# Layer 1's weight splits moved into layer 0, and its output projection woven into its attention

## The chip, the cores and the metric

The kernel runs on one core of one Trainium2 chip. A core has TensorE (PE in the profile, PEld for its weight loads), VectorE (DVE), ScalarE (ACT), GpSimd (POOL) and SyncE (SP). SP's, ACT's and POOL's queues start DMA transfers; 16 DMA engines carry them. The metric is the device time of one execution in microseconds, and less is better.

## The reference

Two layers, 1024 positions, 1024 channels. A layer mixes positions, adds the input times a constant, normalises, applies a squared-ReLU MLP of width 4096, and normalises again. Layer 0 mixes with gated linear attention (GLA) and with multi-head latent attention (MLA, causal, 8 heads). Layer 1 mixes with a sparse attention that keeps the 256 best keys of each query by an index score (DSA), and with a state-space part (S5) whose result passes a gate (GLU). Cut to what matters:

```python
for i in range(DEPTH):
    if i % 2 == 0:   # [GLA, MLA] @ w_out
        mix = _mixer_gla_mla(x, positions, *mixer_params[i])
    else:            # [DSA, S5 with GLU] @ w_out
        mix = _mixer_dsa_s5(x, *mixer_params[i])
    x = _layernorm(DEEPNORM_ALPHA * x + mix, ln1_g, ln1_b)
    x = _layernorm(DEEPNORM_ALPHA * x + _sq_relu_mlp(x, w1, w2), ln2_g, ln2_b)

# _mixer_dsa_s5
q, k, v, qi, ki, wi, u = _split(x @ w_in, L1_SPLITS)
o_dsa = _dsa(q, k, v, qi, ki, wi * IDX_HEADS ** -0.5)   # top-k by index score, softmax, @ v
y = gelu(_s5(u, ...));  o_s5 = y * sigmoid(y @ glu_w + glu_b)
return concatenate([o_dsa, o_s5], -1) @ w_out
```

## The kernel before

**Numbers in two parts.** A float32 factor is held as a high part that TensorE's fast format (fp32r) takes exactly and a low part, the rest. A product is three passes: high by high, high by low, low by high. Whoever wants to multiply first splits: ACT copies the high part, DVE or POOL subtracts it from the value. For weights `unit` (L617) does this. It loads a block of 128 x 1024 (`wr`, 512 KB) on SP's queue and makes four tiles of 128 x 512: `wh`, `wl` for the left half, `wh`, `wl` for the right.

**Stages.** `program` (L2135 on) goes through layer 0's projections, GLA and MLA attention (until about 440 us), its output projection `out_norm` with `l0_wo` (440 to 560), the MLP as `fc1` and `fc2` with seven products in place of eight (560 to about 1160), then layer 1: the index scores and the selection (`index`, `topk`), the projections `l1_in` (L1673), DSA in two halves of queries of 16 steps each, S5 and GLU beside it (until about 1640), `out_norm` with `l1_wo`, and the MLP again. In the attentions one step handles two blocks of 128 queries of one head (32 steps in MLA): products for the scores into PSUM, a maximum on DVE (`SM`), the exponential on ACT (`p`), transposes on TensorE (`ident,p`), a split of the transposed block (`pth` on ACT, `ptl` on DVE), the products with the values (`vv`).

**What sets the order.** Nothing is issued directly. A class records every operation, a list scheduler with a cost for each operation puts them in order for each engine, and one line (L471) then issues all. So all rows of the profile carry L471, and operations are told apart by their tiles. What is recorded together can be interleaved: `program` runs several generators side by side, some steps of one for each step of another, by the numbers in the tables at L2102 to L2117 (E0, E1, GL, GS for S5 and GLU beside DSA; SKEW for the order of `out_norm`, which starts with six blocks of the first half of the positions). An operation assigned to 'E' goes to DVE or POOL, as the scheduler decides. Each queue is in order: what stands behind a waiting instruction waits too, and a DMA's issue takes its place in the queue of its engine.

**The names that the prediction uses.** `wr`, `wh`, `wl` (weights raw, high, low); `pth`, `ptl`, `p`, `SM`, `vv`, `fold`, `rs` (attention; `rs` is a block's row sums, transposed once for each pair of heads and half of the positions, eight times in MLA); `ir` (index scores in ACT); `jv`, `ja` (counting passes of the selection on DVE and ACT); `mh`, `ml` (the mixed result, the input of `out_norm`); `iq`, `qkl` (low parts of projections).

Of the kernel before, what the change touches and what calls it, by code (L numbers as in the profile page):

```python
# [11 lines left out]
F32 = mybir.dt.float32  # L12
F32R = mybir.dt.float32r
# [460 lines left out]
P, T, N, KD = 128, 1024, 512, 8  # L474
# [26 lines left out]
def run(g, n=None):  # L501

    for i, _ in enumerate(g):
        if n is not None and i + 1 >= n:
            return


def weave(main, *others):

    for _ in main:  # L510
        for o in others:
            run(o, 1)
    for o in others:
        run(o)


class Kern:
    def __init__(self, ctx, tc, A, out, dbg=None, drams=None, at=None, made=None):

        self.tc, self.A, self.out, self.at = tc, A, out, at  # L520
        self.dbg, self.drams = dbg or {}, drams
        self.uid = 0
        self.DF = self.DS = self.ZE = 0
        self.MG = 1
        nc = self.nc = Plan(tc.nc)
        self.V, self.S, self.G, self.TE = nc.vector, nc.scalar, nc.gpsimd, nc.tensor
        self.E, self.H = Either(nc, nc.vector, nc.gpsimd), Either(nc, nc.scalar, nc.vector)
        e = ctx.enter_context
        sb, ps = e(tc.tile_pool(name="sb", bufs=1)), e(tc.tile_pool(name="ps", bufs=1, space=PSUM))
        self.pool, self.tiles = {"SB": sb, "PS": ps}, {}  # L530
        if at is not None:
            self.room = {w: p.tile([P, n // 4], F32, name=w) for w, p, n in
                         (("SM", sb, SMALL), ("PS", ps, 8 * PAGE))}
            for name, (w, o) in at.items():
                if w in ("SB", "BG"):
                    shape, dt = made[name]
                    self.tiles[name] = sb.tile(shape, dt, name=name, tag=f"{w}{o}")
# [78 lines left out]

    def unit(self, dram, he=None, le=None):  # L617

        raw = self.big(name="wr")
        self.nc.sync.dma_start(out=raw, in_=dram)  # L620
        u = []
        for i in range(2):
            wh, wl = self.slab(F32R, "wh"), self.slab(F32R, "wl")
            self.split(raw[:, i * N:(i + 1) * N], wh, wl, self.by("unit_h"), self.by("unit_l"))
            u.append((wh, wl))
        return u

    @staticmethod
    def cut(u, c, n=P):
# [555 lines left out]
        yield from self.attention([item(hd, h) for hd in range(8) for h in range(2)])  # L1185


    def out_norm(self, wname, mix, res, g, b, emit):

        V = self.V  # L1190
        us, st = {}, [{}, {}]
        for k, h in self.skewed(KD, 0, SKEW):
            if k not in us:
                us[k] = self.unit(self.A[wname][k])
            ps = self.ps1()
            self.dense(mix, h, ps, lambda kk: self.blk(us[k], kk))
# [393 lines left out]
    def topk(self, blocks, on_act, sc, hi16, lo16, bias):  # L1590
# [70 lines left out]
        for j, qb in enumerate(blocks):  # L1661
# [8 lines left out]
            bias[qb] = b  # L1670
            yield

    def l1_in(self, x, dq, dk, dv, du):  # L1673

        V, S, A, nc = self.V, self.S, self.A, self.nc
        W = A["l1_fm"]
        us = [self.unit(A["l1_v"][i]) for i in range(4)]
        for b in range(8):
            ps = self.ps1((P, 8, 64))
            bs = slice((b % 4) * P, (b % 4 + 1) * P)  # L1680
            self.tm(us, lambda k: tuple(t[:, bs] for t in x[k][b // 4]), ps)
            for hg in range(2):
                v = self.slab(F32R, "vv", (P, 4, 2, 64))
                for par in range(2):
                    src = ps[:, hg * 4 + par:hg * 4 + 4:2, :]
                    hs, ls = v[:, par::2, par, :], v[:, par::2, 1 - par, :]
                    self.copy(S, hs, src)
                    V.tensor_tensor(ls, src, hs, ALU.subtract)
                nc.scalar.dma_start(out=dv[b, hg], in_=v.rearrange("p a b c -> p (a b c)").bitcast(F32))
            yield  # L1690
        us = [self.unit(A["l1_u"][i]) for i in range(4)]
        for h in range(2):

            uq = [self.slab(name="ut", shape=(P, 8, 4, 16)) for _ in range(4)]
            for j in range(4):
                ps = self.ps1((P, 4, 8, 16))
                self.tm(us, lambda k: tuple(t[:, j::4] for t in x[k][h]), ps)
                for q in range(4):
                    self.copy(S, uq[q][:, :, j, :], ps[:, q])
                    if j == 3:  # L1700
                        nc.scalar.dma_start(out=du[q, h], in_=uq[q].rearrange("p a b c -> p (a b c)"))
                yield
# [374 lines left out]
    def glu(self, y, mix):  # L2077
# [10 lines left out]
        for h in range(2):  # L2088
            for ct in range(4):
# [12 lines left out]
RUSH, R0, NI, NT, N0, SK, ACTS, SR, E0, E1, DF, DS, E2, I2, MV, GL, GS, CI, CS, CJ, DF0, DS0, MC, WV, RO, ZE = 800, 300, 6, 2, 4, 1, (4, 7), -100, 2, 2, 0, 0, 2, 14, 3, 5, 1, 2, 2, 3, 0, 0, 4, 3, 7, 1  # L2102
# [6 lines left out]
BY = {'unit_h': 'S', 'unit_l': 'E', 'loadx_h': 'S', 'loadx_l': 'V', 'glao_h': 'S', 'glao_l': 'G', 'mlac_h': 'S', 'mlac_l': 'V', 'mlaq_h': 'S', 'mlaq_l': 'G', 'mlao_h': 'S', 'mlao_l': 'E', 'half_h': 'S', 'half_l': 'V', 'fc1_h': 'S', 'fc1_l': 'E', 'dsao_h': 'S', 'dsao_l': 'G', 'x2_h': 'H', 'x2_l': 'V', 'y_h': 'H', 'y_l': 'G', 'glu_h': 'H', 'glu_l': 'V', 'lnacc': 'G', 'lnsq': 'G', 'gla': 'G', 'gdl': 'G', 'gor': 'G', 's5u': 'V', 's5a': 'G', 's5m': 'G', 's5n': 'G', 's5t': 'G', 's5g': 'G', 'lo16': 'V', 'hi16': 'V'}  # L2109
# [25 lines left out]
def program(K, A, out, stop=None):  # L2135
    V, S, G, nc = K.V, K.S, K.G, K.nc

    def tables(name):
        S.preload_act_table_set(name)
# [5 lines left out]
    x, us = pairs(), {}  # L2145
# [47 lines left out]
    K.out_norm("l0_wo", mix, res0, "l0_ln1_g", "l0_ln1_b", K.keep("x1", op, dx))  # L2193
    if stop == "x1":
        return
    x2 = pairs()
# [56 lines left out]
        if i >= I2 and (i - I2) % E2 == E2 - 1:  # L2253
            run(s5, 1)
    run(top0)
    for i, _ in enumerate(K.dsa(dq, dk, dv, bias, mix, 0)):
        run(top1, NT)
        if i % E0 == E0 - 1:
            run(s5, 1)
    run(top1)  # L2260
    glu = K.glu(ys, mix)
    for i, _ in enumerate(K.dsa(dq, dk, dv, bias, mix, 1)):
        if i % E1 == E1 - 1:
            run(s5, 1)
        if i >= GL:
            if i == GL:
                run(s5)
            run(glu, GS)
    K.DF = K.DS = 0
    run(s5)  # L2270
    run(glu)
    if stop == "mix1":
        return
    tables("natural_log_exp_and_others")
    op = {i: [None] * 4 for i in range(1, 8)}
    K.out_norm("l1_wo", mix, res1, "l1_ln1_g", "l1_ln1_b", K.keep("x3", op, dx))

    def last(h, c, k, t):
        nc.sync.dma_start(out=out[k, :, h * N + c.start:h * N + c.stop], in_=t)
# [90 lines left out]
```

## Time and profile before

| | |
|---|---|
| time, median of 3 runs | 2386.18 us (2385.55 to 2389.04) |
| profiled execution | 2386.76 us, span 2384.6 us |
| mean granted TensorE clock | 0.991 |
| PE busy | 2299.7 us (96%) |
| DVE, ACT, POOL busy | 1765.8, 1330.2, 468.3 us |
| `wr` loads for `unit` in layer 1's mixer | 23 of 512 KB |

The span runs from the first to the last instruction; the execution's time is 2.2 us more. All times in rows are from the start of the span. A share of busy time is a mean over stages with different limits, so stages are read one by one.

### The profile page before, as it was taken

The numbers are of one execution on the slowest core, as the hardware profiler recorded it, in microseconds if no ns is written. First come the engines' busy times: TensorE is split into PE (matmuls) and PEld (weight loads), VectorE is DVE, ScalarE is ACT, GpSimd is POOL, SyncE is SP. The second block draws the span as 40 slices with busy tenths as digits, with TensorE's granted clock in tenths as the row PEclk, the third lists the DMA queues.
The fourth block names the chain that finished last, engine by engine and source line by source line (L and its number), as shares of the span: only waits on it lengthen the run. The fifth ranks groups of instructions, "written<-read, shape, count | busy, mean of one in ns | idle before, by whom it ended". The sixth has DMA issues, their size and how long they took to land. (4 is left out here: it accounts for less than half of the span.)

```text
span 2384.6 us, 33342 instructions
## 1 busy us (share of the span) xinstructions
PE 2299.7 (96%) x11356; PEld 1904.9 (80%) x11356; DVE 1765.8 (74%) x3345; ACT 1330.2 (56%) x2649; POOL 468.3 (20%) x487
## 2 busy tenths in 40 slices
PE   8999999999999999999999997899999999999997
PEld 7787888887788788887778976788878787888887
DVE  9676778468775567578899989985597755675795
ACT  4365667347555554446578775884275454544462
POOL 1252332232000000003211335742320000000021
PEclk9999999999999999999999998999999999999998
DMA  5420002225554585665203569563155546765561
GB/s 187 166 80 1 1 1 63 89 80 164 198 172 152 191 306 186 203 199 195 69 33 115 160 194 282 151 168 116 54 167 195 166 152 203 250 244 187 187 218 36
DMA packets 174940, 356.59 MB, mean 150 GB/s; under 512 B 26785, under 2 KB 39345, under 8 KB 174769
## 3 DMA queue, kind: packets, MB, share of 16 engines
q1 hardware_dynamic: 111280, 244.33, 32.2%
q10 hardware_dynamic: 50816, 87.05, 9.8%
q0 software_dynamic: 12672, 23.07, 3.5%
q8 instruction: 89, 1.46, 0.3%
q14 instruction: 83, 0.67, 0.1%
HBM read 249.66 MB, written 104.73 MB: 149 GB/s over the span
## 5 line engine op out<-in xcount | busy, mean ns | idle before, releaser
L471 PE MATMUL PS<-bh,wb 128*128 128x512 f32 x1792 | 566.6, 394 | 14.6 <-ACT u L471 7.1
L471 PEld LDWEIGHTS PS<-bh,wb 128*128 128x128 f32 x1792 | 334.8, 188 | 104.4 <-ACT u L471 12.7
L471 PE MATMUL PS<-bl,wb 128*128 128x512 f32 x896 | 349.6, 390 | 0.0
L471 PE MATMUL PS<-gl,vh 128*128 128x512 f32 x832 | 325.9, 392 | 2.1 <-DVE gl L471 2.1
L471 PE MATMUL PS<-gh,vl 128*128 128x512 f32 x832 | 325.4, 392 | 0.0
L471 PE MATMUL PS<-gh,vh 128*128 128x512 f32 x832 | 323.1, 392 | 0.3 <-DVE res L471 0.2
L471 PEld LDWEIGHTS PS<-bl,wb 128*128 128x128 f32 x896 | 168.5, 188 | 33.9
L471 PEld LDWEIGHTS PS<-gl,vh 128*128 128x128 f32 x832 | 157.1, 189 | 35.6 <-DVE gl L471 2.8
L471 PEld LDWEIGHTS PS<-gh,vh 128*128 128x128 f32 x832 | 156.7, 189 | 34.8 <-ACT vh L471 1.0
L471 PEld LDWEIGHTS PS<-gh,vl 128*128 128x128 f32 x832 | 157.3, 189 | 32.8
L471 POOL TENSOR_TENSOR wl<-wr,wh 128x512 fp32r<-128x512 f32 x77 | 122.2, 1603 | 248.3 <-ACT wh L471 168.2
L471 PE MATMUL PS<-xh,wh 128*128 128x512 f32 (+1 forms) x400 | 154.6, 391 | 15.0 <-ACT wh L471 6.9
L471 ACT ACTIVATE c<-c 128x512 f32<-128x512 f32 x224 | 140.7, 630 | 49.7 <-DVE c L471 42.8
L471 POOL TENSOR_TENSOR lnacc<-res,res 128x512 f32<-128x512 f32 (+1 forms) x8 | 9.8, 1226 | 768.8 <-DVE res L471 768.8
L471 DVE TENSOR_TENSOR gl<-hr,gh 128x512 fp32r<-128x512 f32 x208 | 148.9, 717 | 11.6 <-PE PS L471 5.7
L471 ACT ACTIVATE gh<-hr 128x512 fp32r<-128x512 f32 x208 | 129.2, 623 | 50.2 <-PE PS L471 33.9
L471 PE MATMUL PS<-xh,wl 128*128 128x512 f32 (+1 forms) x400 | 153.4, 386 | 2.0 <-POOL wl L471 2.0
L471 PE MATMUL PS<-xl,wh 128*128 128x512 f32 (+1 forms) x400 | 155.0, 388 | 0.0
L471 ACT ACTIVATE wb<-wf 128x512 fp32r<-128x512 f32 x96 | 59.7, 628 | 154.3 <-DMA wf<-in_l_w 94.1
L471 DVE TENSOR_TENSOR wb<-s,wb 128x512 fp32r<-128x512 f32 x128 | 87.8, 688 | 74.8 <-ACT wb L471 74.7
L471 DVE TENSOR_TENSOR vl<-s,vh 128x512 fp32r<-128x512 f32 x112 | 84.8, 760 | 77.7 <-ACT vh L471 39.4
L471 ACT ACTIVATE vh<-s 128x512 fp32r<-128x512 f32 x112 | 70.3, 629 | 108.4 <-PE PS L471 72.1
(367 smaller groups left out, 5479.3 us busy)
## 6 DMA issues: line engine op xcount, KB each, us to landing
wr<-in_l_w SPq DMA_DIRECT2D x118, 512.0 KB, 5.1
hr<-hd SPq DMA_DIRECT2D x208, 256.0 KB, 3.4
wf<-in_l_w SPq DMA_DIRECT2D x80, 512.0 KB, 3.8
hd<-t ACTq DMA_DIRECT2D x128, 256.0 KB, 2.7
hd<-c ACTq DMA_DIRECT2D x96, 256.0 KB, 2.3
wr<-in_l_fm SPq DMA_DIRECT2D x25, 512.0 KB, 5.2
wr<-in_l_wo SPq DMA_DIRECT2D x16, 512.0 KB, 4.5
dx<-res ACTq DMA_DIRECT2D x32, 256.0 KB, 2.3
```

The costliest lines, as they stand in the source:

```text
L471: r = getattr(queue.real, method)(*a, **k)
```

## The change

**Splits ahead of time.** A new generator `prepare` takes the 23 weight blocks of layer 1's mixer (13 of `l1_fm`, 4 of `l1_v`, 4 of `l1_u`, 2 of `glu`), loads and splits each with `unit` as before, and stores the four parts (256 KB each) in DRAM (`dw`) from ACT's queue: 92 stores. It runs beside layer 0: one block for each step of MLA's attention from step 20 on, then two for each step of layer 0's `out_norm`. When `unit` is asked for one of these blocks in layer 1, it loads the four parts from `dw` on SP's queue (92 loads) and splits nothing.

**The output projection woven in.** `out_norm` becomes a generator with its order given. For layer 1 the order is all eight blocks of the first half of the positions, then all eight of the second, and the weights `l1_wo` are loaded and split once for each half (8 more loads of 512 KB, 16 more copies, 16 more subtractions). The first half is run two steps at a time beside the last four of DSA's 32 steps, and the change of ACT's table stands ahead of it there.

**Numbers.** S5 steps beside DSA come every 4th step in the first half (every 2nd before) and every 3rd in the second; GLU starts at step 5 of the second half, as before (GL counts from the first half now); `glu_l` goes from DVE to POOL; FAR 4 to 5, SKEW 6 to 5. The number of products is unchanged.

```diff
     def unit(self, dram, he=None, le=None):
 
+        if not hasattr(dram, "ap"):
+            dram = dram[tuple(slice(None) for _ in dram.shape)]
+        at = self.ready.get((dram.tensor.name, dram.offset))
+        if at is not None:
+            u = [tuple(self.slab(F32R, n) for n in ("wh", "wl")) for _ in range(2)]
+            for i in range(4):
+                self.nc.sync.dma_start(out=u[i // 2][i % 2].bitcast(F32), in_=at[i])
+            return u
         raw = self.big(name="wr")
...
+    def prepare(self, blocks, to):
+
+        for n, dram in enumerate(blocks):
+            for i, t in enumerate(t for half in self.unit(dram, self.by("pre_h"), self.by("pre_l")) for t in half):
+                self.nc.scalar.dma_start(out=to[n, i], in_=t.bitcast(F32))
+            yield
+        for n, dram in enumerate(blocks):
+            self.ready[dram.tensor.name, dram.offset] = to[n]
...
-    def out_norm(self, wname, mix, res, g, b, emit):
+    def out_norm(self, wname, mix, res, g, b, emit, order, again=False):
...
-        for k, h in self.skewed(KD, 0, SKEW):
-            if k not in us:
-                us[k] = self.unit(self.A[wname][k])
+        for k, h in order:
+            u = k, h if again else 0
+            if u not in us:
+                us[u] = self.unit(self.A[wname][k])
...
+            yield
...
-... E0, E1 ... = ... 2, 2 ...  GL = 5
+... E0, E1 ... = ... 4, 3 ...  GL = 21
+AGAIN, UFIRST = True, False   
+PRE, PA, PB, PC = 23, 20, 1, 2
+WO, WS, WR = 28, 2, 0   
-BEGUN, FAR = 4, 4
+BEGUN, FAR = 4, 5
-SKEW = 6
+SKEW = 5
...
-    weave(m or first, g)
+    pre = K.prepare(blocks, K.dram("dw", [len(blocks) or 1, 4, P, N]))
+    for i, _ in enumerate(m or first):
+        run(g, 1)
+        if i >= PA:
+            run(pre, PB)
+    run(g)
...
+    for _ in K.out_norm("l0_wo", mix, res0, "l0_ln1_g", "l0_ln1_b", K.keep("x1", op, dx), K.skewed(KD, 0, SKEW)):
+        run(pre, PC)
+    run(pre)
...
+            if i >= WO:
+                if i == WO:
+                    run(s5)
+                    run(glu)
+                    tables("natural_log_exp_and_others")
+                n = min(WS, (KD if AGAIN else KD - SKEW) - done)
+                if n > 0:
+                    nc.rush = WR
+                    run(wo, n)
+                    nc.rush = 0
+                    done += n
```

ACT's queue in layer 0's attention, before, a few rows behind the fourth of the eight `rs` (`fold` and `qh` belong to the steps of another head):

```order
L471 ACTIVATE pth_6062<-PS 128x512
L471 ACTIVATE pth_6054<-PS 128x384
L471 ACTIVATE fold_6066<-PS 64x512
L471 ACTIVATE qh_6068<-q_6067 128x512
L471 ACTIVATE pth_6063<-PS 128x384
L471 ACTIVATE p_6070,SM<-PS,SM 128x384
```

And the same place with the change:

```order
L471 ACTIVATE pth_6205<-PS 128x512
L471 ACTIVATE pth_6192<-PS 128x384
L471 DMA dw<-wl_6202 128x512
L471 DMA dw<-wh_6199 128x512
L471 DMA dw<-wl_6201 128x512
L471 ACTIVATE wh_6210<-wr_6186 128x512
L471 DMA dw<-wh_6200 128x512
L471 ACTIVATE wh_6211<-wr_6189 128x512
L471 DMA dw<-wh_6210 128x512
L471 ACTIVATE wh_6214<-wr_6189 128x512
L471 ACTIVATE fold_6216<-PS 64x512
L471 ACTIVATE qh_6218<-q_6213 128x512
```

Between the copies of the transposed block and `fold` now stand three copies of layer 1's weights and five stores of their parts; from this `rs` to the last of the eight there are 68 stores and 36 `wh` copies in this queue, where 14 copies stood.

TensorE's order near the end of DSA's second half, before: the products with the values of one block, and the transposes of the next:

```order
L471 MATMUL PS<-pth_8297,vv_8133 128x256
L471 MATMUL PS<-ptl_8304,vv_8133 128x256
L471 MATMUL PS<-pth_8297,vv_8137 128x256
L471 MATMUL PS<-ptl_8304,vv_8137 128x256
L471 MATMUL PS<-ident,p_8288 128x128
L471 MATMUL PS<-ident,p_8291 128x128
L471 MATMUL PS<-ident,p_8288 128x128
L471 MATMUL PS<-ident,p_8291 128x128
```

And with the change, products of `l1_wo` (`mh`, `ml` by `wh`, `wl`) ahead of such transposes:

```order
L471 MATMUL PS<-mh_8417,wh_8524 128x512
L471 MATMUL PS<-ml_8427,wh_8524 128x512
L471 MATMUL PS<-mh_8417,wl_8529 128x512
L471 MATMUL PS<-mh_8433,wh_8524 128x512
L471 MATMUL PS<-ml_8438,wh_8524 128x512
L471 MATMUL PS<-mh_8433,wl_8529 128x512
L471 MATMUL PS<-ident,p_8561 128x128
L471 MATMUL PS<-ident,p_8563 128x128
L471 MATMUL PS<-ident,p_8561 128x128
```

These are the last of 35 products in a row; 153 products of `l1_wo` stand ahead of the last product with values in the whole order, where 13 did.

## Rows read from the trace of the kernel before

**Rows 1.** The page: each engine's busy us (share of the span) xinstructions.

```profile
PE 2299.7 (96%) x11356; PEld 1904.9 (80%) x11356; DVE 1765.8 (74%) x3345; ACT 1330.2 (56%) x2649; POOL 468.3 (20%) x487
```

**Rows 2.** By stretch: us; PE, PEld, DVE, ACT, POOL busy; PEclk; DMA share, GB/s.

```profile
340.00:440.00 100.00, 98.62 (x654) 84.21 (x654) 81.64 (x143) 80.12 (x181) 33.18 (x57) 1.00 0.22 69
440.00:560.00 120.00, 119.31 (x538) 97.89 (x537) 68.49 (x103) 44.70 (x81) 39.22 (x28) 1.00 0.30 97
...
1175.00:1300.00 125.00, 116.53 (x531) 95.42 (x531) 122.14 (x278) 99.91 (x222) 23.23 (x21) 1.00 0.19 66
1300.00:1425.00 125.00, 121.81 (x566) 106.21 (x566) 112.46 (x268) 98.37 (x251) 35.35 (x26) 1.00 0.57 170
1425.00:1550.00 125.00, 102.59 (x623) 84.18 (x623) 115.15 (x281) 82.48 (x191) 83.02 (x97) 0.95 0.75 212
1550.00:1640.00 90.00, 88.84 (x569) 78.26 (x568) 80.86 (x202) 74.70 (x144) 39.79 (x47) 1.00 0.54 159
1640.00:1750.00 110.00, 110.00 (x494) 90.37 (x493) 58.12 (x88) 36.91 (x68) 37.23 (x26) 1.00 0.26 88
```

**Rows 3.** What TensorE waited for, 1100 to 1640: total us, times, longest.

```profile
PE PS L471 <- ACT ir L471: 5.6, 6, 1.5
PE PS L471 <- ACT wh L471: 5.5, 3, 3.7
PE PS L471 <- DVE ptl L471: 5.2, 9, 1.5
PE PS L471 <- ACT p L471: 3.3, 5, 1.1
...
PE PS L471 <- POOL wl L471: 2.0, 3, 1.0
```

**Rows 4.** By stretch, layer 0 from the fourth to the last `rs` transposes.

```profile
353.10:438.00 84.90, 84.01 (x558) 71.78 (x557) 69.51 (x110) 67.14 (x145) 24.56 (x44) 1.00 0.26 82
```

**Rows 5.** ACT by operation, 353 to 438: busy us, mean ns, idle before.

```profile
L471 ACT ACTIVATE p<-PS,SM 128x384 f32<-128x384 f32 (+7 forms) x30 | 22.9, 768 | 5.9 <-DVE SM L471 5.8
...
L471 ACT ACTIVATE wh<-wr 128x512 fp32r<-128x512 f32 x15 | 8.8, 628 | 1.6 <-DMA wr<-in_l_wo 1.6
```

**Rows 6.** ACT in time order at stores: start us, us, engine (ACTq: queue), what.

```profile
730.30 1.72 ACTq L471 DMA_DIRECT2D hd<-t  x3
732.06 0.63 ACT L471 ACTIVATE wb<-wf 128x512 fp32r<-128x512 f32 x1 [1.52 <-PE PS L471]
...
1190.36 1.15 ACT L471 ACTIVATE res<-res 128x512 f32<-128x512 f32 x2
1191.00 0.33 ACTq L471 DMA_DIRECT2D dr<-res  x1
1191.47 0.63 ACT L471 ACTIVATE res<-res 128x512 f32<-128x512 f32 x1
...
1200.14 0.93 ACTq L471 DMA_DIRECT2D dr<-res  x2
1201.12 0.63 ACT L471 ACTIVATE wh<-wr 128x512 fp32r<-128x512 f32 x1 [0.40 <-DVE sc L471]
```

**Rows 7.** Splits by tile, 1075 to 1550: ns min/median/max, starts.

```profile
L471 DVE TENSOR_TENSOR wl<-wr,wh x9: 679/692/1773, 1154.8 to 1418.7; 128x512 fp32r<-128x512 f32 x9
```

**Rows 8.** The page: 40 slices of the span, DMA busy tenths and GB/s.

```profile
DMA  5420002225554585665203569563155546765561
GB/s 187 166 80 1 1 1 63 89 80 164 198 172 152 191 306 186 203 199 195 69 33 115 160 194 282 151 168 116 54 167 195 166 152 203 250 244 187 187 218 36
```

**Rows 9.** DVE 1100 to 1425, ACT 1100 to 1640, by operation.

```profile
L471 DVE TENSOR_TENSOR wl<-wr,wh 128x512 fp32r<-128x512 f32 x9 | 7.4, 826 | 5.6 <-ACT wh L471 5.6
...
L471 ACT ACTIVATE wh<-wr 128x512 fp32r<-128x512 f32 x62 | 36.6, 624 | 17.6 <-DMA wr<-in_l_fm 14.7 <-DMA wr<-in_l_u 1.1 <-DVE vl L471 0.8
```

**Rows 10.** The page: DMA issues, KB each, median us from issue to landing.

```profile
hr<-hd SPq DMA_DIRECT2D x208, 256.0 KB, 3.4
...
wr<-in_l_fm SPq DMA_DIRECT2D x25, 512.0 KB, 5.2
```

More of the change, by code (lines that the diff above doesn't have):

```diff
@@ L523, in __init__ @@
         self.DF = self.DS = self.ZE = 0
+        self.ready = {}
         self.MG = 1
@@ L623, in unit @@
             wh, wl = self.slab(F32R, "wh"), self.slab(F32R, "wl")
-            self.split(raw[:, i * N:(i + 1) * N], wh, wl, self.by("unit_h"), self.by("unit_l"))
+            self.split(raw[:, i * N:(i + 1) * N], wh, wl, he or self.by("unit_h"), le or self.by("unit_l"))
             u.append((wh, wl))
         return u
+    def prepare(self, blocks, to):
[5 more added lines that the diff above has]
+            self.ready[dram.tensor.name, dram.offset] = to[n]
     @staticmethod
@@ L1185, in mla @@
         yield from self.attention([item(hd, h) for hd in range(8) for h in range(2)])
-    def out_norm(self, wname, mix, res, g, b, emit):
+    def out_norm(self, wname, mix, res, g, b, emit, order, again=False):
         V = self.V
         us, st = {}, [{}, {}]
-        for k, h in self.skewed(KD, 0, SKEW):
-            if k not in us:
-                us[k] = self.unit(self.A[wname][k])
+        for k, h in order:
+            u = k, h if again else 0
+            if u not in us:
+                us[u] = self.unit(self.A[wname][k])
             ps = self.ps1()
-            self.dense(mix, h, ps, lambda kk: self.blk(us[k], kk))
+            self.dense(mix, h, ps, lambda kk: self.blk(us[u], kk))
             z, f = res(k, h)
@@ L1671, in topk, with l1_u @@
             yield
+    def l1_u(self, x, du):
+        S, A, nc = self.S, self.A, self.nc
+        us = [self.unit(A["l1_u"][i]) for i in range(4)]
+        for h in range(2):
+            uq = [self.slab(name="ut", shape=(P, 8, 4, 16)) for _ in range(4)]
+            for j in range(4):
+                ps = self.ps1((P, 4, 8, 16))
+                self.tm(us, lambda k: tuple(t[:, j::4] for t in x[k][h]), ps)
+                for q in range(4):
+                    self.copy(S, uq[q][:, :, j, :], ps[:, q])
+                    if j == 3:
+                        nc.scalar.dma_start(out=du[q, h], in_=uq[q].rearrange("p a b c -> p (a b c)"))
+                yield
     def l1_in(self, x, dq, dk, dv, du):
@@ L1676, in l1_in @@
         W = A["l1_fm"]
+        if UFIRST:
+            yield from self.l1_u(x, du)
         us = [self.unit(A["l1_v"][i]) for i in range(4)]
@@ L1690, in l1_in @@
             yield
[L1691 to L1702, printed above, removed]
+        if not UFIRST:
+            yield from self.l1_u(x, du)
         for pr in range(4):
@@ L2101, in glu @@
                 yield
-RUSH, R0, NI, NT, N0, SK, ACTS, SR, E0, E1, DF, DS, E2, I2, MV, GL, GS, CI, CS, CJ, DF0, DS0, MC, WV, RO, ZE = 800, 300, 6, 2, 4, 1, (4, 7), -100, 2, 2, 0, 0, 2, 14, 3, 5, 1, 2, 2, 3, 0, 0, 4, 3, 7, 1
+RUSH, R0, NI, NT, N0, SK, ACTS, SR, E0, E1, DF, DS, E2, I2, MV, GL, GS, CI, CS, CJ, DF0, DS0, MC, WV, RO, ZE = 800, 300, 6, 2, 4, 1, (4, 7), -100, 4, 3, 0, 0, 2, 14, 3, 21, 1, 2, 2, 3, 0, 0, 4, 3, 7, 1
 RO = [(["r0", "r1", "r2", "r3", "cq0", "cq1", "ckv"], 4), (["cq0", "cq1", "ckv", "r0", "r1", "r2", "r3"], 4), (["cq0", "cq1", "ckv", "r0", "r1", "r2", "r3"], 3),
  (["r0", "r1", "cq0", "cq1", "ckv", "r2", "r3"], 4), (["r0", "r1", "cq0", "cq1", "ckv", "r2", "r3"], 5), (["r0", "cq0", "cq1", "ckv", "r1", "r2", "r3"], 4), (["r0", "r1", "r2","cq0", "cq1", "ckv",  "r3"], 4), (["r0", "r1", "r2","cq0", "cq1", "ckv",  "r3"], 6)][RO]
-BY = {'unit_h': 'S', 'unit_l': 'E', 'loadx_h': 'S', 'loadx_l': 'V', 'glao_h': 'S', 'glao_l': 'G', 'mlac_h': 'S', 'mlac_l': 'V', 'mlaq_h': 'S', 'mlaq_l': 'G', 'mlao_h': 'S', 'mlao_l': 'E', 'half_h': 'S', 'half_l': 'V', 'fc1_h': 'S', 'fc1_l': 'E', 'dsao_h': 'S', 'dsao_l': 'G', 'x2_h': 'H', 'x2_l': 'V', 'y_h': 'H', 'y_l': 'G', 'glu_h': 'H', 'glu_l': 'V', 'lnacc': 'G', 'lnsq': 'G', 'gla': 'G', 'gdl': 'G', 'gor': 'G', 's5u': 'V', 's5a': 'G', 's5m': 'G', 's5n': 'G', 's5t': 'G', 's5g': 'G', 'lo16': 'V', 'hi16': 'V'}
+BY = {'pre_h': 'S', 'pre_l': 'E', 'unit_h': 'S', 'unit_l': 'E', 'loadx_h': 'S', 'loadx_l': 'V', 'glao_h': 'S', 'glao_l': 'G', 'mlac_h': 'S', 'mlac_l': 'V', 'mlaq_h': 'S', 'mlaq_l': 'G', 'mlao_h': 'S', 'mlao_l': 'E', 'half_h': 'S', 'half_l': 'V', 'fc1_h': 'S', 'fc1_l': 'E', 'dsao_h': 'S', 'dsao_l': 'G', 'x2_h': 'H', 'x2_l': 'V', 'y_h': 'H', 'y_l': 'G', 'glu_h': 'H', 'glu_l': 'G', 'lnacc': 'G', 'lnsq': 'G', 'gla': 'G', 'gdl': 'G', 'gor': 'G', 's5u': 'V', 's5a': 'G', 's5m': 'G', 's5n': 'G', 's5t': 'G', 's5g': 'G', 'lo16': 'V', 'hi16': 'V'}
+AGAIN, UFIRST = True, False
+PRE, PA, PB, PC = 23, 20, 1, 2
+WO, WS, WR = 28, 2, 0
 BACK, SQUARE = 1, 1
@@ L2175, in program @@
             first, m = m, None
-    weave(m or first, g)
+    blocks = [A["l1_fm"][i] for i in (4, 0, 1, 2, 3)] + [A[n][i] for n in (("l1_u", "l1_v") if UFIRST else ("l1_v", "l1_u")) for i in range(4)]
+    blocks += [A["l1_fm"][i + j] for i in range(4) for j in (5, 9)] + [A["glu"][i] for i in range(2)]
+    blocks = blocks[:PRE]
+    pre = K.prepare(blocks, K.dram("dw", [len(blocks) or 1, 4, P, N]))
[4 more added lines that the diff above has]
+    run(g)
     if stop == "mix0":
@@ L2192, in program @@
     op = {i: [None] * 4 for i in range(1, 8)}
-    K.out_norm("l0_wo", mix, res0, "l0_ln1_g", "l0_ln1_b", K.keep("x1", op, dx))
+    for _ in K.out_norm("l0_wo", mix, res0, "l0_ln1_g", "l0_ln1_b", K.keep("x1", op, dx), K.skewed(KD, 0, SKEW)):
+        run(pre, PC)
+    run(pre)
     if stop == "x1":
@@ L2255, in program @@
     run(top0)
[L2256 to L2260, printed above, removed]
-    glu = K.glu(ys, mix)
[L2262 to L2268, printed above, removed]
+    glu = K.glu(ys, mix)
+    op = {i: [None] * 4 for i in range(1, 8)}
+    wo = K.out_norm("l1_wo", mix, res1, "l1_ln1_g", "l1_ln1_b", K.keep("x3", op, dx),
+                    [(k, h) for h in range(2) for k in range(KD)] if AGAIN else K.skewed(KD, 0, SKEW), AGAIN)
+    begun, done = False, 0
+    for h in range(2):
+        if h:
+            run(top1)
+        for i, _ in enumerate(K.dsa(dq, dk, dv, bias, mix, h), 16 * h):
+            if not h:
+                run(top1, NT)
+            if i % E0 == E0 - 1:
+                run(s5, 1)
+            if i >= GL:
+                if i == GL:
+                    run(s5)
+                run(glu, GS)
+            if i >= WO:
+                if i == WO:
+                    run(s5)
+                    run(glu)
[6 more added lines that the diff above has]
+                    done += n
     K.DF = K.DS = 0
@@ L2273, in program @@
         return
-    tables("natural_log_exp_and_others")
-    op = {i: [None] * 4 for i in range(1, 8)}
-    K.out_norm("l1_wo", mix, res1, "l1_ln1_g", "l1_ln1_b", K.keep("x3", op, dx))
+    if WO > 31:
+        tables("natural_log_exp_and_others")
+    run(wo)
     def last(h, c, k, t):
```

## Prediction

> **What bounds the kernel now.** I read the page's busy table first: TensorE is busy 2299.7 of 2384.6 us, so at most 85 us of this time is open idle, and ACT and DVE are bounds only inside single stages [rows 1]. So the second view is the table of busy time by stretch [rows 2]. The reader is to see two different situations in it. In layer 0's MLA attention (340 to 440) TensorE is busy 98.62 of 100 us, and in the output projection behind it 119.31 of 120: nothing waits there, and ACT, at 80.12 and then 44.70, has the room. In layer 1's projections, selection and attention (the four stretches from 1175 to 1640) TensorE is idle 8.47, 3.19, 22.41 and 1.16 us; DVE is busy 122.14 of 125 us at first and 115.15 of 125 later. In 1425 to 1550 the granted clock is 0.95 on top. The third view, what TensorE waited for between 1100 and 1640, gives the idle time its names [rows 3]: 5.6 us for ACT's `ir`, 5.5 for ACT's weight copies `wh`, 2.0 for POOL's `wl`, and some ten for the attention's own chain (`ptl`, `p`, `qkl`). The change takes weight splitting out of the second situation and puts it into the first.
>
> **The change part by part.** Durations are from the profiled execution, 2386.76 us; the median of the runs is 2386.18, so I take 0.6 off at the end.
>
> *Layer 0's attention, the price.* From the fourth to the last of its eight row-sum transposes (353.1 to 438.0) it lasts 84.9 us, with TensorE busy 84.01 and ACT 67.14 [rows 4]. By the instruction order of both kernels, ACT's queue there now holds 36 `wh` copies where 14 stood, and 68 of the 92 stores. A copy is 628 ns by itself [rows 5], and 0.55 us where activations of this size follow each other (two in the 1.11 us from 1190.36 to 1191.47, [rows 6]): 22 x 0.55 = 12 us, so ACT needs 79 of 84.9 us before any store. Of the 68 stores 16 stand alone and the rest in 8 pairs, 4 threes and 6 fours. The price of a store comes from other places of the trace [rows 6]. One alone, at 1191.00, lies beside a running activation, and the next begins at 1191.47, without a gap: 0. A pair leaves 0.40 us idle before the next activation, three leave 1.52; four, at 0.6 us for one more, 2.1 (an estimate from these). So 8 x 0.4 + 4 x 1.5 + 6 x 2.1 = 22 us, and ACT needs 101 us in a stretch of 85: +16 if ACT never waits. It does wait (5.9 us in front of `p`, [rows 5]), and a store of a `wl` has to wait for the subtraction on DVE or POOL, with the exponentials and `pth` copies, on which TensorE depends, queued behind it. I take **+18**. The lower bound is +2, if every store rides under an activation as the lone one does; the upper is +35, all 68 at 0.60 us (41 us, ACT at 120).
>
> The rows say that stores on ACT's queue cost ACT time. The Trainium skill (DMA: Bandwidth & Descriptors, "Issuing engines are not separate DMA queues") says that issuing from several engines saves only the sequencer's time to initiate a DMA, "usually small relative to the DMA itself", and its latency table gives about 50 ns for the dispatch. By that, 68 stores would be an estimated 3.4 us, ACT would need 82 of 85 us, and the stretch would not grow. The 1.72 us that three take in the row speak against it. The first rival below is where the rule would hold.
>
> *DVE, POOL, SP and transfers there.* DVE is busy 69.51 of 84.9 us and takes most of the added subtractions; at 0.69 us each (the median of DVE's own `wl`, [rows 7]), about 20 would bring it to 83, below ACT's 101, so nothing is added for it. On SP's queue 13 raw loads now precede the first of `l0_wo`, and the `l0_wo` copies come behind the added ones on ACT; TensorE reaches that weight directly behind its last product. With 120 us of projection for the following blocks, I take **+2** for the first (bounds 0 and 5). The 24 remaining stores fall where ACT is busy 44.70 of 120 us [rows 2]: 0, covered by TensorE's 119.31; without that cover, 14 us. The transfers: 23 raw blocks (12 MB) and 68 parts (18 MB) come to the 7 MB that go at 82 GB/s now [rows 4]; 37 MB in 103 us are 359 GB/s, beyond the fastest slice of the page, 306 GB/s at a share of eight tenths [rows 8]. This I keep for a rival.
>
> *Layer 1's projections, the gain.* 23 blocks no longer need 46 copies and 46 subtractions there. TensorE's direct waits for them, 5.5 and 2.0 us, go: 7.5 [rows 3]. DVE is the pace in this part: its nine `wl` are 7.4 us and the idle time in front of them is 5.6 [rows 9]; TensorE is not behind DVE all the time, so I count half, 6.5. ACT stood 17.6 us in front of `wh`, mostly for raw weights [rows 9]; that the `ir` behind them come earlier I count at 3 of the 5.6 us. Together **-17**; bounds -7.5 (the named waits alone) and -24 (DVE's 13 us whole). Late next: DVE's counting passes for the selection, which stay, and `p`, `ptl`.
>
> The parts come as 92 loads of 256 KB instead of 23 of 512 KB, 12 MB more. A 512 KB block lands in 5.2 us after its issue, a 256 KB one in about 3.4 [rows 10], and nothing computes between landing and use any more. **+1** (bounds 0 and 5, a late part in front of the first products).
>
> *First half of layer 1's attention.* In 1425 to 1550 TensorE is idle 22.41 us and at 0.95 of the clock, which costs up to 0.05 x 125 = 6 more. The change moves S5 steps from here to the second half and takes POOL's splitting away, but the chain of softmax blocks is what TensorE waits for (`ptl` 5.2, `p` 3.3, [rows 3]), and that stays. **-6** (bounds 0 and -12).
>
> *The weave.* By the order, 153 products of `l1_wo` now stand ahead of the last attention product where 13 stood: 140 x 0.223 (494 in 110 us behind it, [rows 2]) = 31 us of projection moves into the last four steps. They can fill only what is open: 1.16 us of idle in 1550 to 1640, and the narrow products there that wait on each other without showing as idle. Reading `l1_wo` a second time adds 16 copies (10 us of ACT) where ACT has 15 us left in 90. **-5** (bounds +3 and -10).
>
> *Knobs.* Where the S5 and GLU steps fall is in the two terms above; `glu`'s low part moves 8 subtractions from DVE to POOL, and SKEW and FAR shift a few blocks: 0 each, covered by TensorE at 110 of 110 us behind the attention.
>
> Sum: +18 + 2 - 17 + 1 - 6 - 5 = -7. 2386.8 - 7 - 0.6 = **2379.2 us**.
>
> **The rivals.**
>
> *Stores ride free.* The order lists stores in groups, but ACT may reach them spread out, with its own waits (17 us in this stretch) hiding them. Then layer 0 costs +2 and the sum is -23: 2363. For it: the lone store's price of 0. Against: 79 us of copies before any store, and the groups of three with 1.5 us.
>
> *Transfers pace ACT.* The page's fastest slices are 306 GB/s at a share of eight tenths and 282 at nine. If 37 MB go at 313 GB/s (282 over 0.9), the stretch takes 118 us: +33. A store that lands late keeps its `wh` and `wl` buffers, the next copy into them stands in ACT's queue, and the exponentials stand behind it. Sum: 33 + 2 - 28 + 1 = +8: 2394. It decides for slower from a price of +30 in layer 0 on. Against: the split work can drift behind into the projection, where transfers are few.
>
> *Layer 1 gives back only named waits.* DVE is busy 122 of 125 us with the selection, so what its queue loses in splits it spends waiting for ACT's counts, and the attention chain stays. Then -7.5 and -2 for the weave, with +21 of price: +11.5, or 2398. For it: DVE's share in 1175 to 1425, nearly all of it selection, since its `wl` are 7.4 us of it. Against: the idle time in front of its `wl` is real and ends.
>
> *The two cancel.* Price +18, with layer 1's return at 18 to 22 instead of 28: +1, 2387. In this case the change only moves time.
>
> **How the numbers follow.** Forecast 0.40, free stores 0.20, transfers 0.14, only named waits 0.12, cancel 0.14. Within 0.2% (about what a measurement of this kernel can tell from no change) is 2381.4 to 2391. The forecast's own range, 2371 to 2387, lies faster in 0.26 of the 0.40 and within it in 0.14. With free stores 0.20 faster. The slower rivals give 0.21 slower and 0.05 within, cancel 0.08 within, 0.02 faster and 0.04 slower. Faster 0.48, same 0.27, slower 0.25. As cases of both signs hold much of the chance, the range reaches from 2358 (free stores and the gains' far ends) to 2399 (the named waits alone).
>
> **What would show it.** Right: layer 0's stretch between the fourth and the last `rs` transposes takes about 103 us instead of 84.9, with ACT near its full busy or issuing time and TensorE waiting for ACT's `p` and `pth`; no TensorE waits on `wh` and `wl` from 1100 to the end of the projections; that part 17 us shorter; the two halves of attention 11 us shorter together with the woven products taken off. Wrong: a stretch of about 87 us (stores free); TensorE waiting for a DMA or `wh` behind SP (transfers); layer 1's part shorter by under 10 us, with the same DVE busy share. The prediction falls if the price in layer 0 is outside 5 to 28 us or layer 1's return outside 18 to 38.

## The result: slower by 23 us, where 7 us less were forecast

The changed kernel takes 2409.14 us (2407.29 to 2410.36, 4 runs) against 2385.86 us of the kernel before on the same chip: a ratio of 1.0086, 95% interval 1.007 to 1.0102. The forecast was 2379.2 with a range from 2358 to 2399: the time moved the other way, and it lies outside the range.

The page after, against [rows 1] and [rows 8]:

```profile
PE 2306.4 (96%) x11356; PEld 1911.4 (79%) x11356; DVE 1780.3 (74%) x3375; ACT 1336.2 (56%) x2660; POOL 444.3 (18%) x478
...
DMA  5420017843455568456523579754245546665561
GB/s 185 165 79 1 1 55 254 305 167 132 151 203 166 185 227 311 150 184 206 182 93 117 173 246 280 215 171 137 101 139 188 177 149 214 229 248 189 188 223 36
```

The span is 21 us longer and TensorE's busy time 7, for the same number of products, so 14 us of the difference are idle time and 7 go to a lower clock (0.986 on average, 0.991 before). Most of it arises where the DMA row changed: the 6th to 9th slices (301 to 541 us) show 1, 7, 8 and 4 tenths where 0, 2, 2 and 2 stood. The stretches of layer 0 and the projections of layer 1 (busy times of PE, PEld, DVE, ACT, POOL; granted clock; DMA share, GB/s), against [rows 2, 4]:

```profile
355.30:468.00 112.70, 91.67 (x555) 75.19 (x553) 75.76 (x116) 77.67 (x166) 42.20 (x61) 0.94 0.77 271
468.00:566.00 98.00, 91.95 (x406) 75.29 (x405) 56.20 (x79) 31.85 (x59) 28.33 (x19) 0.97 0.44 162
1196.00:1470.00 274.00, 267.82 (x1281) 230.55 (x1280) 252.35 (x595) 195.41 (x468) 39.64 (x47) 1.00 0.53 169
```

The stretch from the fourth to the last `rs` transposes takes 112.7 us, 27.8 more. TensorE is idle for 21 us of it, and its clock falls to 0.94: around idle times of 4.6 and 7.4 us it was granted the lower of its two levels, 1.2 in place of 2.4 GHz, for 14 us. ACT is busy 77.67, and its stores are in issue for 31.4 us, of which 13.9 lie outside its activations. So for 21.1 us of the 112.7 it neither computes nor issues (17.8 of 84.9 before), and for 9.0 of these a store at the head of its queue waits for the landing of a transfer, as shown below. The stretch did not become ACT-bound in the sense of the prediction (busy or issuing all the time). What TensorE and ACT waited for there:

```profile
PE PS L471 <- ACT p L471: 14.6, 6, 7.4
PE PS L471 <- ACT pth L471: 4.8, 4, 2.6
PE PS L471 <- ACT qh L471: 1.0, 1, 1.0
```

```profile
ACT p L471 <- DMA wr<-in_l_fm: 5.4, 1, 5.4
ACT wh L471 <- PE PS L471: 3.8, 4, 1.5
ACT qh L471 <- DMA dw<-wh: 3.5, 1, 3.5
ACT wh L471 <- DMA wr<-in_l_fm: 3.0, 1, 3.0
```

TensorE waits for ACT's exponentials (14.6 us; before, all its idle time in this stretch was 0.9 us, [rows 4]), and ACT's exponential waits for the DMA of a raw weight block, `wr`, that it never reads. One such place in order of time, ACT first and then SP's queue:

```profile
446.01 0.63 ACT L471 ACTIVATE wh<-wr 128x512 fp32r<-128x512 f32 x1 [0.72 <-ACT wh L471]
446.28 5.73 ACTq L471 DMA_DIRECT2D dw<-wh  x2
452.06 0.69 ACT L471 ACTIVATE p<-PS,SM 128x512 f32<-128x512 f32 x1 [5.42 <-DMA wr<-in_l_fm]
```

```profile
445.12 0.33 SPq L471 DMA_DIRECT2D wr<-in_l_fm  x1
...
446.29 0.96 SPq L471 DMA_DIRECT2D wr<-in_l_fm  x1
```

Two stores stand behind the copy of 446.01. The first is issued at 446.28, the second only at 451.69, and the exponential behind it starts at 452.06, after 5.42 us in which ACT stood idle. In the records of the trace the second store has in front of it a wait for a semaphore that ends at 451.65. The raw block issued at 445.12 landed at 451.61. Store and block share no tile. This is no single case: of the 92 stores, 30 stood at the head of ACT's queue for longer than 0.3 us, 30.8 us together. 19 of these waits, 23.8 us together, end within 0.05 us after the landing of a transfer: 13 times a load of `wr` or `res`, 6 times another store.

The records also show what is waited for. A transfer tells its landing on a semaphore, a counter that others can wait for. SP's and ACT's transfers use eight of them between the two queues, and a queue does not issue a transfer before the one that used the same semaphore last has landed. The store of 451.69 uses number 106, and its last user was the raw block of 445.12. In all 19 waits the landing is that of the last user of the store's own semaphore. In the traces of all 18 kernels here no transfer starts before the last one on its semaphore has landed, and SP and ACT together reach eight transfers in flight in each and never pass them. POOL's transfers use eight other semaphores. So a store in ACT's queue can wait for a load in SP's, and the exponentials wait with it. The wait is an instruction of the program in ACT's queue, so this is how its transfers are set up; nothing here shows it to be a limit of the chip.

Where the 20.9 us of span come from, read at the same products in both traces: +2.2 ahead of 355 us; +27.8 in the attention; +9.4 in `l0_wo`'s projection and the MLP's first part; -26.6 from there to the end of layer 1's projections; +0.7 in the first half of DSA; +2.6 in the second half with `l1_wo`; +5.8 in the first part of layer 1's MLP; -1.0 behind it. The first and last products of the MLP's first part in layer 0 (`bl`, 400 to 1000 us; ns min/median/max, first and last start) are the mark by which the experiments read the price in layer 0, before layer 1 can mix in; before and after:

```profile
L471 PE MATMUL PS<-bl,wb x448: 387/389/402, 526.6 to 866.9; 128*128 128x512 f32 x150
```

```profile
L471 PE MATMUL PS<-bl,wb x448: 387/389/403, 566.5 to 906.3; 128*128 128x512 f32 x150
```

866.9 and 906.3: the price is 39.4 us. The mark comes from one profile of each run, but it repeats where layer 0 is the same or nearly so: 905.5 and 907.4 (e1, e5) beside 906.3, and 865.9 (e16) beside 866.9. (One correction to the description of the change: the number E1 is set but not read any more. S5 comes every fourth step in both halves of DSA.)

### The profile page after: what moved, and what is told of

It is laid out like the page before. It is cut to its first block, busy times and chain, and to the rows that moved or that the text cites. A ratio compares the mean times of both kernels' runs of the same rounds, so it can differ in the third digit from the quotient of the medians.

```text
span 2405.5 us, 33793 instructions
## 1 busy us (share of the span) xinstructions
PE 2306.4 (96%) x11356; PEld 1911.4 (79%) x11356; DVE 1780.3 (74%) x3375; ACT 1336.2 (56%) x2660; POOL 444.3 (18%) x478
## 3 DMA queue, kind: packets, MB, share of 16 engines
q10 hardware_dynamic: 64064, 111.18, 12.4%
## 5 line engine op out<-in xcount | busy, mean ns | idle before, releaser
L471 PEld LDWEIGHTS PS<-gh,vh 128*128 128x128 f32 x832 | 156.2, 188 | 34.7 <-issue 0.9
L471 ACT ACTIVATE wb<-s 128x512 fp32r<-128x512 f32 x128 | 80.3, 627 | 93.4 <-PE PS L471 67.8
L471 POOL TENSOR_TENSOR lnacc<-lnacc,res 128x512 f32<-128x512 f32 (+1 forms) x40 | 56.0, 1400 | 393.4 <-DVE res L471 387.6
L471 POOL TENSOR_TENSOR wl<-wr,wh 128x512 fp32r<-128x512 f32 x66 | 97.0, 1480 | 166.3 <-ACT wh L471 120.7
```

The costliest lines, as they stand in the source:

```text
L471: r = getattr(queue.real, method)(*a, **k)
```

## The experiments

The theories at the start: **issue**, stores and copies cost time in ACT's queue; **transfers**, the bytes load the DMA engines until blocks and buffers come late. Any edit lets the planner order layer 1 anew. In e1, e2 and e3 the products behind the mark are the same as before in another order, and from the mark to the first product of layer 1's MLP they take 10, 23 and 16 us more in the profiled runs. So prices in layer 0 are read at the mark (last `bl`), not from the whole time; this was settled when e1 to e3 had run.

**e1, the price alone.** `prepare` runs, nobody reads; all numbers as before, no weave:

```diff
-            self.ready[dram.tensor.name, dram.offset] = to[n]
+            pass
```

> The 23 blocks are loaded, split and stored in layer 0 exactly as in the changed kernel, but nobody reads the stored parts: layer 1, its weave and the knobs are those of the kernel before. It measures the price in layer 0 by itself. Both theories (issue: stores and copies cost time in ACT's in-order queue; transfers: loads and stores together load the DMA engines so that raw blocks, buffers and the projection's own weights come late) expect what the trace of the changed kernel shows, some 38 us over the kernel before, 2424 us. Under 2405 the price would come from layer 1's side after all.

2426.42 us, ratio 1.0166 (1.0138 to 1.0193); mark at 905.5, +38.6. The price is layer 0's.

**e2, an eighth of the bytes.**

```diff
-                self.nc.scalar.dma_start(out=to[n, i], in_=t.bitcast(F32))
+                self.nc.scalar.dma_start(out=to[n, i][:16], in_=t.bitcast(F32)[:16])
```

> As e1, but each of the 92 stores writes 16 of the 128 partitions: the same number of stores in the same places of ACT's queue, an eighth of their bytes (3 MB in place of 24 MB). If issue is the price, the time stays within 6 us of e1 (about 2420). If transfers are, most of the price goes: the stretch in layer 0's attention falls to 90 to 95 us from 113, and the whole to 2392 to 2400.

2423.35 us, 1.0147 (1.013 to 1.0164). The whole time is within 6 us of e1, as for "issue", and misleads: the mark is at 882.2, +15.3, so 23 of 39 us went with the bytes, and layer 1's new order took as much. The attention took 92.0 us, as expected for "transfers".

**e3, no store** (the store's line is `pass`).

> As e1 without any store: the raw loads, 46 copies and 46 subtractions stay. Issue theory: the stretch needs ACT for 79 us of 85, so 2387 to 2392. Transfer theory: the 12 MB of raw loads alone are well under what the engines carry, the same 2387 to 2394. If the price stays over 15 us here, it is the splitting itself (ACT's copies, or waits in queue order for raw blocks), and both theories are wrong.

2407.02 us, 1.0083 (1.0068 to 1.0098), mark at 872.5, +5.6. The whole time is 19 us over the kernel before, and by the expectation's own words (over 15) that would speak against both theories; by the mark, most of the 19 is layer 1's new order. Loading and splitting cost 6, stores of an eighth of the bytes about 10 more, the rest of the bytes 23. The 10 are not issue alone, nor the 23 waits alone: in e2's trace 14 us of the stores' waits still end with a landing, 30 in e1's, and the issues of the 92 stores last 34 us in e2 and 40 in e1.

**e4, the weave and the numbers alone** (`PRE = 0`).

> The changed kernel without the advance splitting (no block prepared, layer 1 splits its weights as before), with the weave, the double reading of l1_wo and all the knobs. My prediction put the weave at -5 and the knobs at 0: 2381. The changed kernel's trace shows the two attention halves and the projection 3 us longer than before and the following MLP 4 us longer: by that 2390 to 2395.

2394.71 us, 1.0028 (1.0018 to 1.0039): as the second reading had it, not -5.

**e5, advance splitting alone** (numbers as before, no weave).

> The changed kernel's advance splitting, used in layer 1, without the weave, with the numbers of the kernel before (l1_wo read once, S5 every second step). If the weave and its numbers cost what e4 shows alone (+7), this is the changed kernel less about 7: 2402, with layer 0's price of 38 and a return of some 25 us in the projections. If the weave helps once the splits are gone, it is slower than the changed kernel, over 2412.

2408.8 us, 1.0088 (1.0055 to 1.012), mark at 907.4. Without the weave the time is the changed kernel's; the expected 7 us did not come.

**e7, the stores from SP's queue.**

```diff
-                self.nc.scalar.dma_start(out=to[n, i], in_=t.bitcast(F32))
+                self.nc.sync.dma_start(out=to[n, i], in_=t.bitcast(F32))
```

> The changed kernel with the 92 stores issued from SP's queue and not from ACT's: bytes, copies and subtractions as before, no store in front of an exponential. e1 to e3, read at the end of layer 0's first MLP part, split the price as 23 for bytes, 10 for issue, 5 for splitting. If bytes act through the DMA engines wherever they are issued, only the 10 of issue go: about 2399, and layer 0's attention still takes 100 us or more. If the bytes' price acts through ACT's queue (a store that is issued slowly or late holds the exponentials behind it), most of 33 goes: 2376 to 2386, and the attention takes 88 to 92 us.

2393.48 us, 1.0034 (1.0016 to 1.0051). The attention takes 91.2 us:

```profile
354.40:445.60 91.20, 87.94 (x566) 73.47 (x565) 77.82 (x118) 76.77 (x166) 41.80 (x60) 1.00 0.91 326
```

```profile
L471 PE MATMUL PS<-bl,wb x448: 387/389/402, 532.2 to 875.2; 128*128 128x512 f32 x150
```

This decides between the theories. The DMA engines are at 0.91 and 326 GB/s, more than in the changed kernel, and the price is 8.3 us, of which e3 pays 5.6 without any store. From 445 to 475 us the engines are busy all the time (1.02, 380 GB/s), and TensorE is busy 30.00 of 30 us. So bytes cost next to nothing through the engines. They cost when the stores stand in ACT's queue, where their issue and their waits for landings hold up the exponentials.

**e8, spread out** (from MLA's first step on, a block every second step, then one per step of the projection).

> The changed kernel with the same 23 blocks, begun with MLA's first step and one for every second step, so that they spread over about 300 us instead of 150: half the bytes, copies and stores per microsecond. If the price is a bound that is passed only when all comes together (DMA engines at 0.77 of their time, ACT at its limit), it falls to under 15 us: 2375 to 2386. If every store costs its time wherever it stands, the price stays at 30 to 40: 2400 to 2410.

2419.79 us, 1.0131 (1.0096 to 1.0166), mark at 901.6, +34.7. Thinner, it costs nearly the same. Waits of stores that end with a landing are 12 us here (24 in the changed kernel), so they alone do not make up the price.

**e10, beside the MLP.**

```diff
-    run(K.fc1(0, op, hd))
+    for _ in K.fc1(0, op, hd):
+        run(pre, 1)
```

> The changed kernel with the 23 blocks prepared beside layer 0's MLP (one for each of the first MLP part's 16 steps, the rest in the second part) and nothing added to the attention or the output projection. There TensorE is the bound, ACT is half idle and the DMA engines move 150 to 200 GB/s of the 400 that they reached in the changed kernel. If the price was the place, it is under 8 us here: 2370 to 2378. If splitting and storing cost the same anywhere, 2400 or more.

2410.83 us, 1.0098 (1.0065 to 1.0131). `bl` starts at 528.0 and ends at 906.0: the whole price again, in a stage where ACT has far more idle time. There TensorE waits for ACT's copies `u`, 16.5 us where 3.7 stood, and ACT in turn stands in front of landings:

```profile
PE PS L471 <- ACT u L471: 16.5, 9, 5.1
PE PS L471 <- ACT wb L471: 6.2, 7, 2.0
```

```profile
ACT wh L471 <- DMA wr<-in_l_fm: 8.2, 3, 5.4
...
ACT u L471 <- DMA dw<-wh: 4.5, 1, 4.5
```

These are the longest of TensorE's waits here, 5.1 us each: in one, ACT's queue stands until a store has landed, in the other its copy `wh` until the raw block has. The clock is at 0.97 in this part, where it was 1.00. So ACT's load does not set the price. My expectation from "the place" was wrong. How much of this price each kind of wait has was not tried apart.

**e9, the stores from POOL's queue** (`gpsimd` in place of `scalar`).

> The changed kernel with the 92 stores issued from POOL's queue. e7 (SP's queue) took the price of layer 0 from 39 to 8 us at the end of the first MLP part. If what counts is only that no store stands in ACT's queue, it is within 8 us of e7: 2388 to 2402. POOL subtracts, so a store's issue there takes POOL's time: if the queue of any engine that computes pays, the subtractions come late and it is over 2402.

2376.75 us, ratio 0.9949 (0.993 to 0.9969): faster than the kernel before, and than e7. Mark at 873.6, +6.7, about what e3 pays with no store. One issue there is longer than on ACT (542 ns against 326 to 350), and the landings are later still than in the changed kernel (median 6.9 us against 5.1), but TensorE's wait for `p` in the stretch is 2.2 us:

```profile
356.10:445.40 89.30, 86.57 (x567) 73.07 (x566) 83.24 (x133) 77.60 (x167) 53.20 (x105) 1.00 0.84 298
```

```profile
L471 POOL DMA_DIRECT2D dw<-wh x46: 542/542/733, 355.0 to 478.2; - x46
...
DMA to landing us min/median/max: 2.3/6.9/10.4
```

```profile
L471 ACTq DMA_DIRECT2D dw<-wh x46: 326/350/1183, 353.8 to 496.3; - x46
...
DMA to landing us min/median/max: 2.0/5.1/8.5
```

**e13, SP's stores, old numbers, no weave; e16, the numbers alone; e17, SP's stores with the numbers, no weave.**

> e7's stores from SP with the numbers of the kernel before and no weave: advance splitting alone, at its low price. Layer 0 +8, the projections -25, and the attention gives back some 10, as in e5: 2378 to 2384. If the attention gives back all, as DVE's selection is what it waits for, 2386 or more.

2389.09 us, 1.0006 (0.9993 to 1.0019): the attention gives back all.

> The kernel before with only the S5 and GLU numbers of the change (S5 every fourth step, the low part of glu on POOL), no advance splitting, no weave. In e4 the first half of layer 1's attention ended 7 us earlier against the kernel before, and the following parts lost 9 in the second half with the projection and 8 in the MLP. If the gain is the numbers' and the losses the weave's, this is 2376 to 2382; if the numbers only move S5 into the second half, 2386 to 2390.

2384.84 us, 0.9992 (0.9978 to 1.0006): not told apart from no change.

> Advance splitting with its stores from SP, the S5 and GLU numbers of the change, no weave. If the parts add up: +8 in layer 0, -25 in the projections, some +8 given back in the attention, -7 from the numbers: 2368 to 2376, faster than both kernels. If the attention's selection on DVE is the bound behind the projections, 2380 to 2386.

2396.64 us, 1.0036 (1.0022 to 1.005). This is outside both expected ranges. The parts do not add up: it is 7.5 us slower than e13. In e7, e13 and e17 the projections end 9 to 12 us earlier than before, not 20 as in e9, and the attention gives it back. Layer 0's mark is the same in the three, 874.4 to 875.3, and why they fall behind e9 afterwards is open.

The last four take POOL's stores, to see where layer 1's return goes.

**e18, old numbers, no weave; e19, the change's S5 and GLU numbers, no weave.**

> Advance splitting with stores from POOL, no weave, the S5 and GLU numbers of the kernel before. If weave and numbers are worth nothing together, it is within 4 us of e9: 2373 to 2381. If the weave's order by halves loses the 6 us that the MLP of layer 1 shows in e9, it is faster: 2368 to 2373. If the weave fills the attention's gaps, as the prediction had it, slower: 2381 to 2387.

2388.07 us, 1.0014 (1.0006 to 1.0023).

> As e18 with the change's numbers for S5 and GLU, still without the weave. In e16 against the kernel before, the numbers shortened the first half of the attention by 10 us at its end and the whole by 3. If that adds to the advance splitting: 3 to 8 us under e18. If S5 in the second half costs as much as it frees in the first: within 3 us of e18.

2384.67 us, 0.9998 (0.9988 to 1.0008). Advance splitting alone is worth nothing, even at its low price; the numbers give some 3 us, with intervals that just overlap.

**e20, order by halves, not woven** (`WO = 32`).

> As e9, with l1_wo read twice and out_norm ordered by halves, but run behind the attention and not woven into it. If the order by halves costs the MLP its 6 to 8 us (the second half is normalised at the last moment), the MLP of layer 1 keeps that loss here; if the interleaving does, it vanishes. If the weave is worth the 5 us of the prediction, this is 5 slower than e9: 2382; if it is worth nothing, 2374 to 2379.

2377.42 us, 0.9969 (0.9958 to 0.9981). Against e19 this is 7 us faster, with the order of `l1_wo` by halves and the change's FAR and SKEW together, which no run takes apart; the interleaving by hand adds nothing that the intervals of e9 and e20 tell apart. The first product of `l1_wo` starts at 1615 us here and at 1627 in e19, and 26 of its products stand ahead of the attention's last, where 13 did. In the MLP's first part of layer 1, from the first `bl` to the last, it loses as the changed kernel does: 343.0 us before, 350.0 here, 343.6 in e19:

```profile
L471 PE MATMUL PS<-bl,wb x448: 387/389/628, 1724.1 to 2067.1; 128*128 128x512 f32 x150
```

```profile
L471 PE MATMUL PS<-bl,wb x448: 387/389/628, 1711.0 to 2061.0; 128*128 128x512 f32 x150
```

```profile
L471 PE MATMUL PS<-bl,wb x448: 387/389/402, 1723.1 to 2066.7; 128*128 128x512 f32 x150
```

So against e19 it wins 12 us up to the MLP and loses 6 in it. All eight traces with the order by halves take 345.0 to 350.0 us there (mean 347.8), the ten without it 340.2 to 347.2 (343.3), so the loss is nearer 4 to 5. That its first products need both halves normalised, and the second is now normalised last, is a possible reason; it was not tried apart, and FAR, the number of the MLP's far blocks, is 5 in all eight and 4 in all ten.

**e21, begun at MLA's step 8** (`PA = 8`).

> As e9, with the splits begun at MLA's step 8 in place of 20. If the 6 to 8 us that remain in layer 0 come from ACT's copies and DVE's subtractions in too short a time, 3 to 6 us are won: 2371 to 2374. If the splitting costs the same wherever it stands, no change: 2375 to 2379.

2391.71 us, 1.0031 (1.0019 to 1.0042), 15 us slower than e9, 9 of them up to the mark, where both expectations had it as fast or faster. Beginning earlier did not lower the price; the cause was not followed further.

## Why the prediction was wrong

The time is 28 us above the forecast of 7 less. Layer 0 has 19 of them, layer 1's attention, weave and MLP 20, and layer 1's projections give 11 back.

**Layer 0's attention, +18 forecast, +27.8 measured.** This is the step that failed. It priced a store by the time that its issue takes in ACT's queue, from rows where few transfers were in flight [rows 6], and let the added work fill ACT's idle time: 79 us of work, 22 of issue and 2 for waits, 103. Measured are 77.7 of work, 13.9 of issue outside it and 21.1 of waits, 112.7. The work was right, and the issue was too large; the rows that its price came from name other ends for the idle times, `PE PS` for the 1.52 us and `DVE sc` for the 0.40. The waits, sized at 2, are what failed: ACT's idle time did not fill up but grew from 17.8 us, as for 9.0 us of it a store holds the queue until an earlier transfer on its semaphore has landed, a wait that the sum does not have at all. With the stores issued from another queue the price falls from 39 us to 8 and 7 (e7, e9). The prediction named what stands behind a waiting store and only looked for the subtraction as its cause. The whole price of layer 0, 39.4 us, is outside the 5 to 28 at which the prediction was to fall.

**The projection behind, +2 forecast, +9.4 measured.** The 24 stores that I put at nothing "covered by TensorE's 119.31" stand there in front of the copies of `l0_wo` and `mh`, and wait for landings as above: TensorE is idle 6 us of 98 at 0.97 of the clock, where it had 0.7 of 120, and one wait holds nearly all of it:

```profile
PE PS L471 <- ACT mh L471: 6.0, 1, 6.0
```

**The transfers rival** came nearest in layer 0 (+33), had the right sign (its sum, 2394, is 15 us short) and the right queue, and its ground was wrong: engines at 0.91 and 326 GB/s cost at most 8.3 us with the stores on SP (e7). **Free stores** had layer 0 at +2 and is refuted by +27.8; spread out they cost as well (e8).

The changed kernel, e7 and e9 measure 39, 8 and 7 us for the same 92 stores from ACT, SP and POOL. The Trainium skill (DMA: Bandwidth & Descriptors, "Issuing engines are not separate DMA queues") says that issuing from several engines only saves the sequencer's time to start a transfer, usually small beside the transfer; by that alone the three would be nearly equal, and the runs do not agree, since what stands behind an issue in its queue waits as long as the issue does. It also says that all run on the same 16 DMA engines; the traces agree with that so far as the landings stay late from any queue, medians of 5.1, 4.4 and 6.9 us. The 50 ns that the prediction took for the dispatch stand on that page under the path of a transfer issued by GpSimd; here an issue shows as 326 ns or more on ACT and 542 on POOL.

**Layer 1's projections, -16 forecast, -26.6 measured**: the mechanism held, TensorE waits for no `wh` or `wl` there, and its idle time from the mark to the last projection falls from 21.9 to 8.9 us, 13.0, a little less than the forecast; the row of 1196 to 1470 has TensorE busy for 267.82 of 274 us. Most of the rest came by terms that were not in the sum: its clock stood at the lower level for 10 us there before and for none now (some 5 us), and 36 products of S5 moved from here into the attention (some 4 us). Luck made this part larger.

**First half, -6 forecast, +0.7; weave, -5 forecast, +2.6, and +5.8 in the MLP, which I had at 0.** In the first half TensorE's idle time did fall, from 12.4 to 8.9 us, but the granted clock fell as well, from 0.95 to 0.87, and 32 products of S5 came in from the projections, while 24 others went on to the second half. The direct named waits there (`qkl` 3.9, `ptl` 2.3) are not of weights:

```profile
PE PS L471 <- DVE qkl L471: 3.9, 1, 3.9
PE PS L471 <- DVE ptl L471: 2.3, 2, 1.6
```

The weave could fill only 3.2 us of idle time from the second half to the MLP, and 4.6 stand there now. The order by halves ahead of the MLP was a cost that the prediction did not look for at all.

Open: why each new order by the planner moves layer 1 by 10 to 23 us; and what more semaphores for SP's and ACT's transfers would give, which was not tried.

## What to carry to other kernels

A DMA in the queue of an engine on the critical path costs what it may have to wait for, beside what its issue takes. Look which transfer holds the semaphore that it will use. Put stores that nobody reads soon into the queue of an engine that is not waited for, before thinking of bytes. Price a moved DMA by the waits of its whole queue under the traffic of the changed kernel. When a planner reorders everything, compare at marks inside the kernel, since the whole time mixes the edit with the new order.

## What the runs showed of the hardware

256 KB stores from ACT land 2.0 to 8.5 us after issue when many are in flight (median 5.1), against medians of 2.3 to 2.7 for the kernel's stores of this size before. The DMA engines moved 326 GB/s over 91 us (e7), and layer 0 took 8.3 us more, 5.6 of which e3 shows without a store. An issue of such a store showed as 326 ns or more on ACT and 542 on POOL. Over layer 0's attention TensorE's granted clock was 0.94, at 1.2 GHz for 14 us around idle times of 4.6 and 7.4 us, where it was 1.00 before: TensorE was busy 7.7 us longer for about the same products, so some 7 of the 27.8 us of that stretch are the clock's.
